# Strassen's scheme for the input products of a feed-forward layer: 18 of 22 gate and up pairs as seven quarter products

## The chip, the cores and the metric

The kernel runs on one core of a Trainium2 chip. What counts is the time of one execution on the device, in microseconds (us); the median over several runs is given. The core's engines are called by their short names: PE is TensorE (PEld its weight loads), DVE is VectorE, ACT is ScalarE, POOL is GpSimd, and SP is the queue that issues the transfers. PE writes its products into PSUM, which has eight banks; one bank holds one tile of 128 partitions by 512 float32 columns.

## The reference, cut to what matters

Two layers, each a half-step feed-forward network (FFN), a mixer (a convolution module in layer 0, a gated DeltaNet in layer 1), and a second FFN: four FFNs in all. The change touches the two of layer 1. With SEQ = 512 tokens, D_MODEL = 1024 and D_FF = 2816, each computes

```python
def swiglu_ffn(h, w_in, w_out):
    gate, up = jnp.split(h @ w_in, 2, axis=-1)
    return (jax.nn.silu(gate) * up) @ w_out

h = modulated(x, 0)
x = x + FFN_RES_WEIGHT * gate(0) * swiglu_ffn(h, w_ffn_in[i, 0], w_ffn_out[i, 0])
```

The change concerns `h @ w_in` alone: 1024 inputs by 5632 outputs (2816 gates, 2816 ups) for 512 tokens.

## The kernel before, in words

**Precision.** All operands are float32, and every product is made from halves: an operand is rounded to a type that PE takes in one pass (`whi`, `hh`), and the rest is kept beside it (`wlo`, `hl`). `mm3` (L171 to L175) then makes three matmuls for one block of 128 inputs: `whi` by `hh`, `whi` by `hl`, `wlo` by `hh`. Lines L173, L174 and L175 are those three, wherever in the program they are called from.

**Weights.** `load_raw` (L154) issues one transfer on SP for a block of 1024 inputs by 128 outputs (512 KB) into one of three `raw` buffers. `split_w` (L160) makes `whi` on ACT (L164) and `wlo` on DVE (L165), each in one of four buffers. The class `Feed` (L474) runs this as a pipeline: `load` takes the next source, `prep` splits the oldest raw block and issues the next load, `take` gives the oldest split block to PE.

**One FFN.** `ffn` (L493) works through 22 pairs of blocks, pair j being gate block j and up block j (128 gates and 128 ups), in three groups of 7, 7 and 8. `block` (L525) preps the feed, takes one split weight block, and accumulates its 8 input blocks, 24 matmuls of 512 columns, in one PSUM tile `mm`. For each pair the gate block is made, then `glu_a` (L533) takes silu on ACT; the up block is made, then `glu_b` (L537) multiplies on DVE, and `glu_c` (L541) splits the result into `ahi` (ACT) and `alo` (DVE). After a group comes its part of the output product: 8 blocks of 7 or 8 inputs, each added to `x` on DVE (L471, L464). The last two blocks of the last group lie in `tail` (L220), which already makes the next stage's first products, as 256-column halves (`head_k`). So an FFN starts with three blocks made: gate and up of pair 0 and gate of pair 1 (`begun`).

**Order.** Within `ffn` the schedule is written out by hand (`manual_schedule`): every engine, SP included, executes in the order in which the program calls it. The waits between the engines come from the framework, by the tiles that an instruction reads and writes.

**Layer 0** also pumps the modulation weights through DVE during its FFNs; in layer 1 that is over. POOL has nothing to do in the FFNs of layer 1 but one weight split in each tail (L217).

Of the kernel before, what the change touches and what calls it, by code (L numbers as in the profile page):

```python
# [15 lines left out]
P = 128  # L16
T = 512
H2 = T // 2
D = 1024
KT = D // P  # L20
NG = T // P
FF = 2816
NPAIR = FF // P
# [24 lines left out]
CT = [3,5]  # L48
ARB = 3
PAD = (40, 168)  # L50
SNW = 7
XP = ((0, 1), (1, 1), (2, 2), (4, 2), (6, 2))
WARM = (4, 7, 4)
# [54 lines left out]
def trunk_kernel(ctx: ExitStack, tc: tile.TileContext, x_in, c_in, vecs, consts, w_ada, w_st,  # L108
                 w_fi, w_fo, w_glu, w_tz, w_pw, w_dn, w_do, out):
    nc = tc.nc  # L110
    pe, act, dve, pool = nc.tensor, nc.scalar, nc.vector, nc.gpsimd

    keep = ctx.enter_context(tc.tile_pool(name="keep", bufs=1))
    wp = ctx.enter_context(tc.tile_pool(name="wp", bufs=4))
# [15 lines left out]
    def scratch(tag, shape=(P, T), dt=F32, bufs=1):  # L130
        return sc.tile(list(shape), dt, tag=tag, name=nm(tag), bufs=bufs)
# [4 lines left out]
    hh = keep.tile([P, KT, T], F32R, name="hh")  # L136
    hl = keep.tile([P, KT, T], F32R, name="hl")
# [335 lines left out]

    class Feed:  # L474
        def __init__(self, srcs, ready, go):
            self.srcs, self.ready, self.raws = list(srcs), list(ready), []
            for _ in range(3 if go else 0):
                self.load()

        def load(self):  # L480
            if self.srcs:
                src, nk = self.srcs.pop(0)
                self.raws.append((load_raw(src, nk), nk))

        def prep(self):
            if self.raws and len(self.ready) < 4:
                self.ready.append(split_w(*self.raws.pop(0)))
                self.load()

# [3 lines left out]
    def ffn(layer, which, nxt, first=None):  # L493
        sub = 2 * which
        f = layer * 2 + which
        norm = Norm()
        ng = len(GROUPS)
        with tc.tile_pool(name=nm("ffn"), bufs=1) as ap, ExitStack() as ax:
            ap.tile([P, PAD[layer]], F32, tag="pad", name=nm("pad"))
            pump = bool(ada["plan"])  # L500
            rate = APACE[which]
            if pump:
                ada["raw"] = ax.enter_context(tc.tile_pool(name=nm("adar"), bufs=2))
            done = SNW if first else len(edge["w"])
            srcs, starts = [], []
            j0 = 0
            for n in GROUPS:
                starts.append(j0)
                srcs += [(w_fi[f, i], KT) for i in range(max(2 * j0, done), 2 * (j0 + n))]
                srcs += [(w_fo[f, m, :, j0:j0 + n, :], n) for m in range(KT)]  # L510
                j0 += n
            srcs += [(s, KT) for s in (nxt[2][:2] if nxt else [])]
            feed = Feed(srcs, [] if first else edge["w"][len(edge["ps"]):], not first)
            begun = first(f, ap, feed) if first else edge["ps"]
            region = ax.enter_context(ExitStack())
            region.enter_context(tc.manual_schedule(engines=ENG))
            box = {}
            for _ in range(2):
                feed.prep()

            def step(n):
                if pump:
                    ada_step(n)

            def block(nk, mhi, mlo):  # L525
                feed.prep()
                w = feed.take()
                ps = mm_tile()
                for k in range(nk):
                    mm3(ps, w, k, mhi[:, k, :], mlo[:, k, :], k == 0, k == nk - 1)  # L530
                return ps

            def glu_a(g):  # L533
                box["s"] = s = scratch("sil", bufs=2)
                act.activation(s, g, AF.Silu)  # L535

            def glu_b(u):  # L537
                box["pr"] = pr = scratch("t", bufs=2)
                dve.tensor_tensor(pr, box["s"], u, ALU.mult)  # L539

            def glu_c(jj):  # L541
                pr = box["pr"]
                act.copy(ahi[:, jj, :], pr)  # L543
                dve.tensor_tensor(alo[:, jj, :], pr, ahi[:, jj, :].bitcast(F32), ALU.subtract)  # L544

            for gi, n in enumerate(GROUPS):
                ahi = ap.tile([P, n, T], F32R, tag="ahi", name=nm("ahi"))
                alo = ap.tile([P, n, T], F32R, tag="alo", name=nm("alo"))
                for jj in range(n):
                    if len(begun) > 1:  # L550
                        g, u = begun.pop(0), begun.pop(0)
                        glu_a(g)
                    else:
                        g = begun.pop(0) if begun else block(KT, hh, hl)
                        step(rate[0])
                        glu_a(g)
                        u = block(KT, hh, hl)
                        step(rate[1])
                    glu_b(u)
                    glu_c(jj)  # L560

                if gi == ng - 1:
                    ev = resid(norm, layer, sub)
                    for m in range(KT - 2):
                        ps = block(n, ahi, alo)
                        step(rate[2])
                        ev(ps, m, full)
                    if pump:
                        ada_drain(which == 1)
                    tail(None, n, ahi, alo, layer, sub, norm, nxt, feed)  # L570
                else:
                    ev = plain_resid(layer, sub)
                    for m in range(KT):
                        ps = block(n, ahi, alo)
                        step(rate[2])
                        ev(ps, m, full)
# [970 lines left out]
    start = ExitStack()  # L1547
# [37 lines left out]
    def begin(f, ap, feed):  # L1585
        stage = ap.tile([P, 4 * D + 2 * SNW * P], F32, tag="ahi", name="stage")
        wst = ap.tile([P, 6 * SNW * P], F32R, tag="alo", name="wst")
        NW = SNW * P
        adas, raws, ws, xn, hf = {}, {}, {}, {}, {}
# [62 lines left out]
        unit(0)  # L1652
        ps = [mm_tile() for _ in range(SNW)]
        lower(0)
        for k in range(KT):
# [132 lines left out]
```

## Time and profile before

| | us |
|---|---|
| median of 3 runs (lowest, highest) | 2051.25 (2049.03, 2054.36) |
| the profiled execution's own time | 2053.78 |
| its span in the profile | 2052.0 |
| PE busy in the span | 1999.5 (97%) |
| DVE, ACT, POOL busy | 1173.2 (57%), 788.8 (38%), 198.6 (10%) |

The profile is one execution. Times are in microseconds from the start of its span unless marked ns. A group's row has the line, the engine, the operation, the output and the inputs with their shapes, the count, then the busy time and the mean duration of one in ns, then the idle time of the engine just before such instructions and what ended it. A timeline row has the start, the duration, the engine, the line and the operation; "x8" marks eight neighbours merged into one row, from the first start to the last end. Matmuls overlap, so the duration of one is longer than the step from one start to the next; the step is what PE can do.

### The profile page before, as it was taken

To read this page: it belongs to the slowest core of one execution; us is meant where nothing else is said; L and a number is where in the kernel's file an instruction comes from. 1 tells how busy PE (TensorE), PEld (TensorE's weight loads), DVE (VectorE), ACT (ScalarE), POOL (GpSimd) and SP (SyncE) were. 2 spreads that over 40 slices of the span, in tenths; PEclk is the share of its full clock that TensorE was granted. 3 is DMA by queue.
4 is the path that set the end of the run, shared out by engine and by line. 5 is a ranking of instruction groups with operands and counts; after the bars stand their busy time and mean duration, and the time that the engine had idled before them with its cause. 6 is when DMAs were issued, how large, how long until landed. Compare 5 with 4: busy or idle time off the path is not lost.

```text
span 2052.0 us, 26228 instructions
## 1 busy us (share of the span) xinstructions
PE 1999.5 (97%) x10355; PEld 1676.0 (82%) x10355; DVE 1173.2 (57%) x1818; ACT 788.8 (38%) x1356; POOL 198.6 (10%) x140
## 2 busy tenths in 40 slices
PE   8999999998899999999999999999899999999998
PEld 6888888877898888889888888887677898888887
DVE  7767666798865656536333333676745664333334
ACT  6422222574642222324222222476656643222222
POOL 0000000299100000000000000024210100000000
PEclk9999999999899999999999999999899999999999
DMA  8767766322236656432332323322111133333331
GB/s 306 233 226 237 229 235 221 104 83 83 78 109 196 210 192 213 162 93 82 98 108 89 106 93 93 113 80 75 62 53 42 51 105 100 106 92 95 102 93 62
DMA packets 78477, 262.06 MB, mean 128 GB/s; under 512 B 8337, under 2 KB 14097, under 8 KB 78226
## 3 DMA queue, kind: packets, MB, share of 16 engines
q1 hardware_dynamic: 77810, 259.87, 39.5%
q8 instruction: 81, 1.33, 0.3%
q10 hardware_dynamic: 544, 0.52, 0.1%
q14 instruction: 42, 0.34, 0.1%
HBM read 254.59 MB, written 5.77 MB: 127 GB/s over the span
## 4 chain that ended last, share of the span: by engine, by line
PE 87%; DVE 5%; POOL 3%; ACT 3%; issue 2%; DMA 0%; SPq 0%; DVEq 0%; POOLq 0%; ACTq 0%
PE mm L173 26%; PE mm L174 26%; PE mm L175 26%; POOL pacc L674 3%; PE mm L1441 1%; PE mm L1463 1%; DVE x L1183 1%; PE aux L378 1%; PE mm L1449 1%; PE mm L1672 1%; PE mm L1673 1%; PE mm L1676 1%; PE mm L1431 1%; DVE t L1104 1%; DVE x L1188 1%
## 5 line engine op out<-in xcount | busy, mean ns | idle before, releaser
L173 PE MATMUL mm<-hh,whi 128*128 128x512 f32 (+1 forms) x1968 | 742.2, 378 | 5.3 <-ACT hh L274 3.6
L174 PE MATMUL mm<-hl,whi 128*128 128x512 f32 (+1 forms) x1968 | 736.7, 375 | 1.6 <-DVE hl L278 1.3
L175 PE MATMUL mm<-hh,wlo 128*128 128x512 f32 (+1 forms) x1968 | 735.0, 374 | 1.9 <-DVE wlo L165 1.9
L165 DVE TENSOR_TENSOR wlo<-raw,whi 128x1024 fp32r<-128x1024 f32 (+1 forms) x291 | 356.0, 1225 | 304.2 <-ACT whi L164 298.1
L173 PEld LDWEIGHTS mm<-hh,whi 128*128 128x128 f32 x1968 | 371.5, 189 | 73.8 <-ACT hh L274 4.4
L175 PEld LDWEIGHTS mm<-hh,wlo 128*128 128x128 f32 x1968 | 372.1, 189 | 68.8 <-DVE wlo L165 2.9
L174 PEld LDWEIGHTS mm<-hl,whi 128*128 128x128 f32 x1968 | 372.3, 189 | 67.3 <-DVE hl L278 3.5
L164 ACT CAST whi<-raw 128x1024 fp32r<-128x1024 f32 (+1 forms) x291 | 297.1, 1022 | 282.2 <-PE mm L174 255.5
L173 PE MATMUL mm<-ahi,whi 128*128 128x512 f32 (+1 forms) x768 | 286.4, 373 | 0.0
L174 PE MATMUL mm<-alo,whi 128*128 128x512 f32 (+1 forms) x768 | 285.7, 372 | 0.0
L175 PE MATMUL mm<-ahi,wlo 128*128 128x512 f32 (+1 forms) x768 | 285.6, 372 | 0.0
L543 ACT CAST ahi<-t 128x512 fp32r<-128x512 f32 x88 | 54.8, 623 | 371.6 <-DVE t L539 371.6
L173 PEld LDWEIGHTS mm<-ahi,whi 128*128 128x128 f32 x768 | 145.2, 189 | 25.2
L174 PEld LDWEIGHTS mm<-alo,whi 128*128 128x128 f32 x768 | 145.2, 189 | 25.0
L175 PEld LDWEIGHTS mm<-ahi,wlo 128*128 128x128 f32 x768 | 145.2, 189 | 24.9
L427 DVE CUSTOM_DVE_ANT_0 ajunk<-araw,cs 128x1024 bf16<-128x1024 f32 x128 | 156.0, 1219 | 0.6
L535 ACT ACTIVATE sil<-mm 128x512 f32<-128x512 f32 x88 | 52.6, 598 | 252.8 <-PE mm L175 252.7
L539 DVE TENSOR_TENSOR t<-sil,mm 128x512 f32<-128x512 f32 x88 | 60.4, 686 | 142.5 <-PE mm L175 140.9
L471 DVE SCALAR_TENSOR_TENSOR x<-mm,gate,x 128x512 f32<-128x512 f32 x64 | 48.1, 751 | 130.2 <-PE mm L175 130.2
L544 DVE TENSOR_TENSOR alo<-t,ahi 128x512 fp32r<-128x512 f32 x88 | 60.9, 692 | 60.6 <-ACT ahi L543 60.6
L217 POOL TENSOR_TENSOR wlo<-raw,whi 128x1024 fp32r<-128x1024 f32 x6 | 14.4, 2393 | 834.0 <-ACT whi L216 834.0
L674 POOL TENSOR_TENSOR pacc<-pacc,pr 128x492 f32<-128x492 f32 (+11 forms) x58 | 83.2, 1435 | 11.4 <-ACT pr L673 7.3
(266 smaller groups left out, 1690.6 us busy)
## 6 DMA issues: line engine op xcount, KB each, us to landing
raw<-in_w_fi_dram SPq DMA_DIRECT2D x169, 512.0 KB, 3.5
araw<-in_w_ada_dram SPq DMA_DIRECT2D x128, 512.0 KB, 4.6
raw<-in_w_fo_dram SPq DMA_DIRECT2D x64, 448.0 KB, 3.4
raw<-in_w_dn_dram SPq DMA_DIRECT2D x33, 512.0 KB, 3.7
raw<-in_w_fo_dram SPq DMA_DIRECT2D x32, 512.0 KB, 3.5
stage<-in_w_ada_dram SPq DMA_DIRECT2D x16, 512.0 KB, 6.4
raw<-in_w_glu_dram SPq DMA_DIRECT2D x16, 512.0 KB, 3.5
raw<-in_w_pw_dram SPq DMA_DIRECT2D x8, 512.0 KB, 3.7
```

What stands on the lines that cost most here:

```text
L164: act.copy(whi[:, :nk, :], raw[:, :nk, :])
L165: dve.tensor_tensor(wlo[:, :nk, :], raw[:, :nk, :], whi[:, :nk, :].bitcast(F32), ALU.subtract)
L173: pe.matmul(ps, whi[:, k, :], mhi, start=first, stop=False)
L174: pe.matmul(ps, whi[:, k, :], mlo, start=False, stop=False)
L175: pe.matmul(ps, wlo[:, k, :], mhi, start=False, stop=last)
L427: dve.tensor_tensor_reduce(junk, raw, ada["cs"], 1.0, 0.0, ALU.mult, ALU.add, accum_out=mod[:, layer, col:col + 1])
L471: dve.scalar_tensor_tensor(x[:, m, sl], ps, gate[:, j:j + 1], x[:, m, sl], ALU.mult, ALU.add)
L535: act.activation(s, g, AF.Silu)
L539: dve.tensor_tensor(pr, box["s"], u, ALU.mult)
L543: act.copy(ahi[:, jj, :], pr)
L544: dve.tensor_tensor(alo[:, jj, :], pr, ahi[:, jj, :].bitcast(F32), ALU.subtract)
L674: pool.tensor_tensor(pacc[m][:, c], pacc[m][:, c], pr[:, c], ALU.add)
```

## The change

In both FFNs of layer 1, pairs 4 to 21 go another way (`LEAD`); pairs 0 to 3 stay as they are. Take the pair's 256 outputs by 1024 inputs by 512 tokens as a product of 2 by 2 quarters: weights g1, g2 (gate, inputs 0 to 511 and 512 to 1023) and u1, u2 (up), activations by input half and by token half (l, r). Seven quarter products replace eight. Each, `prod`, has 4 input blocks by 3 matmuls of 256 columns, that is 12 matmuls. In PE's order, with three PSUM tiles Y, X, Z per pair, and under the names P0 to P6 that the prediction uses:

- P0 into Y's left half: g1 by h(lower, l). ACT copies it out (`p1`).
- P1 into X's left half: the weight sum s1 = u1 + u2 by T0. ACT copies it out (`p5`).
- P2 onto Y's left half: s2 = s1 - g1 by T1. ACT copies the sum out (`u2`).
- P3 into Z's left half: g2 by h(upper, l). DVE adds `p1` to it in place; called ZL here.
- P4 onto Y's left half: s3 = g1 - u1 by T2. ACT copies the sum out (`u3`).
- P5 onto X's left half: s4 = g2 - s2 by h(upper, r).
- DVE writes Y's right half, `u3` + `p5`; called YR here.
- P6 onto Y's left half: u2 by T3. DVE writes Z's right half, X + `u2`; called ZR here. Then silu of Z (`glu_a`), while `glu_b` and `glu_c` are put off (`late`) until after P0 of the next pair.

T0 to T3 are sums of the activations, made once per FFN by `sums_h` in four tasks (each 2 adds of 512 columns on POOL, 4 subtractions of 256 and 2 of 512 columns on DVE, 2 copies on ACT) during pairs 0 to 3. The weight sums of the next pair are made by `sums_w` in four steps, called between the products of the pair before: s1 and s3 on POOL, s2 and s4 on DVE, the splits of g, s1, s2, s3, s4 and u2 on ACT and DVE. Such a pair is called a full pair below. For the last pair of a group the steps prep weights of the output product instead (`feed.prep`); the weight sums for a group's first pair are made during the last two output blocks of the group before, and for pair 4 during pair 3. `Feed` no longer preps a block that is marked for this way (`held`); the last step issues the two next loads.

```diff
+LEAD = {(1, 0): 4, (1, 1): 4}
...
         def prep(self):
-            if self.raws and len(self.ready) < 4:
+            if self.raws and len(self.ready) < 4 and not self.held():
...
             def block(nk, mhi, mlo):
...
+                for _ in range(min(len(side), 1)):
+                    side.pop(0)()
                 return ps
...
+            def sums_h(th, tl):
...
+                    for c in (k, k + KQ):
+                        fs.append(scratch("sq", bufs=2))
+                        pool.tensor_tensor(fs[-1], hh[:, c, :].bitcast(F32), hl[:, c, :].bitcast(F32), ALU.add)
...
+                def first():
+                    st["g"], st["u"] = g, u = feed.pop(), feed.pop()
+                    st["s1"] = s1 = raw_s("pr")
+                    pool.tensor_tensor(s1, u[:, :KQ, :], u[:, KQ:, :], ALU.add)
+                def second():
...
+                    act.copy(gh, g)
+                    dve.tensor_tensor(s2, s1, g[:, :KQ, :], ALU.subtract)
+                    low(gl, g, gh)
+                    act.copy(h1[:, 0], s1)
+                    act.copy(h1[:, 1], s2)
+                def third():
...
+                    pool.tensor_tensor(s3, g[:, :KQ, :], u[:, :KQ, :], ALU.subtract)
+                    act.copy(uh[:, :KQ, :], u[:, KQ:, :])
+                    dve.tensor_tensor(s4, g[:, KQ:, :], s2, ALU.subtract)
+                    low(l1[:, 0], s1, h1[:, 0])
+                    low(l1[:, 1], s2, h1[:, 1])
+                    low(ul[:, :KQ, :], u[:, KQ:, :], uh[:, :KQ, :])
+                    act.copy(h2[:, 0], s3)
+                    act.copy(h2[:, 1], s4)
+                def fourth():
...
+                    low(l2[:, 0], s3, h2[:, 0])
+                    low(l2[:, 1], s4, h2[:, 1])
+                    feed.load()
+                    feed.load()
...
+            def seven(w, th, tl, jj, prep):
...
+                Y, X, Z = mm_tile(), mm_tile(), mm_tile()
+                y, e = Y[:, l], X[:, l]
...
+                prod(0, y, H_(lo4, l), 0)
+                settle()
+                prep[0]()
+                prod(1, e, T_(0), 0)
+                act.copy(p1, y)
+                prep[1]()
+                prod(2, y, T_(1), 1)
+                act.copy(p5, e)
+                prod(3, Z[:, l], H_(hi4, l), 2)
+                act.copy(u2, y)
+                dve.tensor_tensor(Z[:, l], Z[:, l], p1, ALU.add)
+                prep[2]()
+                prod(4, y, T_(2), 1)
+                prod(5, e, H_(hi4, r), 3)
+                act.copy(u3, y)
+                dve.tensor_tensor(Y[:, r], u3, p5, ALU.add)
+                prep[3]()
+                prod(6, y, T_(3), 3)
+                dve.tensor_tensor(Z[:, r], e, u2, ALU.add)
+                glu_a(Z)
+                def rest():
+                    glu_b(Y)
+                    glu_c(jj)
+                late.append(rest)
...
             for gi, n in enumerate(GROUPS):
...
                 for jj in range(n):
+                    if starts[gi] + jj >= lead:
+                        w, nxw = nxw["w"], {}
+                        if jj < n - 1:
+                            prep = sums_w(nxw)
+                        else:
+                            prep = (no, feed.prep, feed.prep, feed.prep)
+                        seven(w, th, tl, jj, prep)
+                        continue
```

## Rows read from the trace of the kernel before

**Rows 1.** The page: the busy time of the engines (us, share of the span, instructions), and the chain of work that ended last.

```profile
PE 1999.5 (97%) x10355; PEld 1676.0 (82%) x10355; DVE 1173.2 (57%) x1818; ACT 788.8 (38%) x1356; POOL 198.6 (10%) x140
PE 87%; DVE 5%; POOL 3%; ACT 3%; issue 2%; DMA 0%; SPq 0%; DVEq 0%; POOLq 0%; ACTq 0%
```

**Rows 2.** Busy time by stretch: the blocks of the two FFNs of layer 1, from the first whole block to the tail. Columns: length, busy time of each engine with the count of its instructions, PE's granted clock (1.00 is full speed, 2.4 GHz), share of the DMA engines, GB/s.

```profile
967.40:1303.00 335.60, 335.60 (x1498) 278.51 (x1497) 128.14 (x137) 94.75 (x118) 0.00 (x0) 1.00 0.33 99
1690.40:2037.00 346.60, 346.60 (x1590) 289.51 (x1588) 131.37 (x146) 96.32 (x123) 0.00 (x0) 1.00 0.30 90
```

**Rows 3.** Timeline of PE: two matmuls of 512 columns that lie 48 matmuls apart, one pair.

```profile
1099.99 0.39 PE L173 MATMUL mm<-hh,whi 128*128 128x512 f32 x1
...
1110.87 0.39 PE L173 MATMUL mm<-hh,whi 128*128 128x512 f32 x1
```

**Rows 4.** Timeline of PE at the start of the first of these FFNs: two matmuls of 256 columns that lie 42 matmuls apart, and the first of the block behind them.

```profile
961.96 0.28 PE L173 MATMUL mm<-hh,whi 128*128 128x256 f32 x1
...
967.00 0.28 PE L173 MATMUL mm<-hh,whi 128*128 128x256 f32 x1
...
967.36 0.40 PE L173 MATMUL mm<-hh,whi 128*128 128x512 f32 x1
```

**Rows 5.** Timeline of DVE at the start of the first of these FFNs: two independent subtractions with nothing between them.

```profile
967.80 2.36 DVE L165 TENSOR_TENSOR wlo<-raw,whi 128x1024 fp32r<-128x1024 f32 x2 [3.41 <-ACT whi L164]
```

**Rows 6.** Groups of instructions of DVE, ACT and POOL over the whole span, each shape apart.

```profile
L165 DVE TENSOR_TENSOR wlo<-raw,whi 128x1024 fp32r<-128x1024 f32 x227 | 286.1, 1262 | 254.0 <-ACT whi L164 250.0
L165 DVE TENSOR_TENSOR wlo<-raw,whi 128x896 fp32r<-128x896 f32 x64 | 69.9, 1092 | 50.2 <-ACT whi L164 48.0
L544 DVE TENSOR_TENSOR alo<-t,ahi 128x512 fp32r<-128x512 f32 x88 | 60.9, 692 | 60.6 <-ACT ahi L543 60.6
L539 DVE TENSOR_TENSOR t<-sil,mm 128x512 f32<-128x512 f32 x88 | 60.4, 686 | 142.5 <-PE mm L175 140.9 <-ACT sil L535 1.5
L273 DVE SCALAR_TENSOR_TENSOR mm<-x,gain,aux 128x256 f32<-128x256 f32 x80 | 38.5, 487 | 3.1 <-PE aux L378 1.5
L407 DVE TENSOR_TENSOR ssum<-ssum,sq 128x256 f32<-128x256 f32 x36 | 15.1, 420 | 8.4 <-ACT sq L402 8.2
...
L164 ACT CAST whi<-raw 128x1024 fp32r<-128x1024 f32 x227 | 236.8, 1045 | 171.9 <-PE mm L174 168.4 <-DMA raw<-in_w_pw_dram 2.1 <-DMA raw<-in_w_fi_dram 1.4
L543 ACT CAST ahi<-t 128x512 fp32r<-128x512 f32 x88 | 54.8, 623 | 371.6 <-DVE t L539 371.6
L535 ACT ACTIVATE sil<-mm 128x512 f32<-128x512 f32 x88 | 52.6, 598 | 252.8 <-PE mm L175 252.7
L897 ACT CAST hh<-sil 128x256 fp32r<-128x256 f32 x16 | 6.5, 408 | 0.5
```

**Rows 7.** Timelines of POOL and DVE in the convolution module, where POOL adds (two operands from SBUF) while DVE subtracts (two operands from SBUF).

```profile
409.58 1.25 POOL L674 TENSOR_TENSOR pacc<-pacc,pr 128x490 f32<-128x490 f32 x1
...
410.91 2.10 POOL L674 TENSOR_TENSOR pacc<-pacc,pr 128x489 f32<-128x489 f32 x1
...
409.88 2.03 DVE L165 TENSOR_TENSOR wlo<-raw,whi 128x1024 fp32r<-128x1024 f32 x1 [0.43 <-ACT whi L164]
```

**Rows 8.** Timelines of PE, ACT and DVE in the DeltaNet, at two PSUM tiles that PE fills in column slices and another engine reads slice by slice: four transposes into `aux` and the first read of its first slice; eight matmuls into `mm` (two for each of four slices) and the first read of its first slice.

```profile
1377.58 0.60 PE L1125 MATMUL aux<-cst,sil 128*128 128x128 f32 x4
...
1378.28 0.28 ACT L1048 ACTIVATE sqj<-aux 128x128 bf16<-128x128 f32 x1
...
1515.95 1.16 PE L1449 MATMUL mm<-sil,kt 64*128 64x128 f32 x8
...
1517.14 0.29 DVE L1452 COPY so<-mm 128x128 f32<-128x128 f32 x1 [4.24 <-PE mm L1449]
```

**Rows 9.** Timelines around three hand-overs: the last matmul of a 256-column block and the DVE instruction that waits for it; a DVE result and the weight load that waits for it; the first two 256-column matmuls after a break.

```profile
937.62 0.28 PE L175 MATMUL mm<-ahi,wlo 128*128 128x256 f32 x1
...
937.95 0.48 DVE L249 SCALAR_TENSOR_TENSOR x<-mm,gate,x 128x256 f32<-128x256 f32 x1 [0.67 <-PE mm L175]
...
1525.13 0.36 DVE L1434 SCALAR_TENSOR_TENSOR sq<-mm,nbe,vb 64x128 f32<-64x128 f32 x1
...
1525.54 0.13 PEld L1441 LDWEIGHTS mm<-sq,rm 64*64 64x64 f32 x1 [0.45 <-DVE sq L1434]
...
943.50 0.36 PE L173 MATMUL mm<-ahi,whi 128*128 128x256 f32 x1
943.71 0.28 PE L174 MATMUL mm<-alo,whi 128*128 128x256 f32 x1
```

**Rows 10.** The page's DMA issues: the weight loads of the input product (count, size of one, median us from issue to landing).

```profile
raw<-in_w_fi_dram SPq DMA_DIRECT2D x169, 512.0 KB, 3.5
```

More of the change, by code (lines that the diff above doesn't have):

```diff
@@ L50 @@
 PAD = (40, 168)
+KQ = KT // 2
+LEAD = {(1, 0): 4, (1, 1): 4}
 SNW = 7
@@ L478, in __init__, with held @@
                 self.load()
+        def held(self):
+            return self.raws[0][1] < 0
         def load(self):
@@ L504, in ffn @@
             done = SNW if first else len(edge["w"])
+            lead = LEAD.get((layer, which), NPAIR)
             srcs, starts = [], []
@@ L508, in ffn @@
                 starts.append(j0)
-                srcs += [(w_fi[f, i], KT) for i in range(max(2 * j0, done), 2 * (j0 + n))]
+                srcs += [(w_fi[f, i], -KT if i >= 2 * lead else KT) for i in range(max(2 * j0, done), 2 * (j0 + n))]
                 srcs += [(w_fo[f, m, :, j0:j0 + n, :], n) for m in range(KT)]
@@ L523, in step @@
                     ada_step(n)
+            side = []
             def block(nk, mhi, mlo):
@@ L544, in glu_c, with task @@
                 dve.tensor_tensor(alo[:, jj, :], pr, ahi[:, jj, :].bitcast(F32), ALU.subtract)
+            def sums_h(th, tl):
+                def task(k):
+                    tf = [scratch("pr", (P, 2, H2), bufs=2) for _ in range(2)]
+                    fs = []
+                    for c in (k, k + KQ):
+                        fs.append(scratch("sq", bufs=2))
+                        pool.tensor_tensor(fs[-1], hh[:, c, :].bitcast(F32), hl[:, c, :].bitcast(F32), ALU.add)
+                    t1, t2, t3, t4 = (tf[i // 2][:, i % 2, :] for i in range(4))
+                    l, r = halves
+                    dve.tensor_tensor(t1, fs[0][:, r], fs[0][:, l], ALU.subtract)
+                    dve.tensor_tensor(t3, fs[1][:, r], fs[0][:, r], ALU.subtract)
+                    dve.tensor_tensor(t2, fs[1][:, r], t1, ALU.subtract)
+                    dve.tensor_tensor(t4, fs[1][:, l], t2, ALU.subtract)
+                    for i in range(2):
+                        c = slice(2 * i, 2 * i + 2)
+                        act.copy(th[:, c, k, :], tf[i])
+                        dve.tensor_tensor(tl[:, c, k, :], tf[i], th[:, c, k, :].bitcast(F32), ALU.subtract)
+                return [lambda k=k: task(k) for k in range(KQ)]
@@ new lines, in ffn, with settle, T_, H_ @@
+            late = []
+            def settle():
+                while late:
+                    late.pop(0)()
+            def seven(w, th, tl, jj, prep):
+                l, r = halves
+                lo4, hi4 = slice(0, KQ), slice(KQ, KT)
+                def T_(i):
+                    return th[:, i], tl[:, i]
+                def H_(ks, sl):
+                    return hh[:, ks, sl], hl[:, ks, sl]
+                def prod(i, ps, m, ends):
+                    (whi, wlo), (mhi, mlo) = w[i], m
+                    for k in range(KQ):
+                        pe.matmul(ps, whi[:, k, :], mhi[:, k, :], start=ends in (0, 2) and k == 0, stop=False, skip_group_check=True)
+                        pe.matmul(ps, whi[:, k, :], mlo[:, k, :], start=False, stop=False, skip_group_check=True)
+                        pe.matmul(ps, wlo[:, k, :], mhi[:, k, :], start=False, stop=ends in (2, 3) and k == KQ - 1, skip_group_check=True)
+                Y, X, Z = mm_tile(), mm_tile(), mm_tile()
+                y, e = Y[:, l], X[:, l]
+                pp = scratch("ssum").rearrange("p (a n) -> p a n", a=2)
+                uu = scratch("t", bufs=2).rearrange("p (a n) -> p a n", a=2)
+                p1, p5, u2, u3 = pp[:, 0], pp[:, 1], uu[:, 0], uu[:, 1]
+                prod(0, y, H_(lo4, l), 0)
[22 more added lines that the diff above has]
+                late.append(rest)
@@ L546, in ffn, with no @@
+            def no():
+                pass
             for gi, n in enumerate(GROUPS):
@@ L548, in ffn @@
                 alo = ap.tile([P, n, T], F32R, tag="alo", name=nm("alo"))
-                for jj in range(n):
+                if gi == 0 and lead < NPAIR:
+                    th = ap.tile([P, 4, KQ, H2], F32R, tag="th", name=nm("th"))
+                    tl = ap.tile([P, 4, KQ, H2], F32R, tag="tl", name=nm("tl"))
+                    side += sums_h(th, tl)
+                    side.pop(0)()
+                    nxw = {}
+                    s4 = sums_w(nxw)
+                    side += [lambda: (s4[0](), s4[1]()), lambda: (s4[2](), s4[3]())]
+                for jj in range(n):
+                    if starts[gi] + jj >= lead:
[6 more added lines that the diff above has]
+                        continue
                     if len(begun) > 1:
@@ L560, in ffn @@
                     glu_c(jj)
+                settle()
                 if gi == ng - 1:
@@ L573, in ffn @@
                     for m in range(KT):
+                        if m == KT - 2 and lead < NPAIR:
+                            nxw = {}
+                            s4 = sums_w(nxw)
+                            side += [lambda: (s4[0](), s4[1]()), lambda: (s4[2](), s4[3]())]
                         ps = block(n, ahi, alo)
```

34 lines of the change are left out of this document (33 added, 1 removed).

## The prediction, made before the changed kernel was run

> **What bounds the kernel now.** I read the page first: PE is busy for 97% of the span and carries 87% of the chain that ended last [rows 1]. Then the stretches that the change touches: in the blocks of both layer-1 FFNs PE is busy for all of 335.6 and 346.6 us, at a granted clock of 1.00, while DVE works 128 and 131 us, ACT 95 and 96, and POOL nothing [rows 2]. So there the time is the number of PE's matmuls times their step, and nothing else waits long enough to matter. The steps come from the timeline. With 512 columns, 48 matmuls, one pair, take 1110.87 - 1099.99 = 10.88 us, 0.2267 each [rows 3]. With 256 columns, 42 matmuls take 967.00 - 961.96 = 5.04 us, 0.120 each [rows 4]: more than half of 0.2267, so part of the scheme's eighth is lost in the halving. Both levels are full clock, and the pauses below are far under a microsecond, so I charge nothing for the clock.
>
> **The change, part by part.**
>
> *PE's own work.* A changed pair is 7 x 12 = 84 matmuls of 256 columns: 84 x 0.120 = 10.08 us against 10.88, a gain of 0.80. Over 18 pairs and two FFNs that would be 36 x 0.80 = 28.8 us. This is the ceiling.
>
> The Trainium skill (TensorE: Matmul & The Clock Gate, Back-to-back issue gap) gives a matmul N / 2.4 + 2.5 ns: 109 ns for 256 columns and 216 ns for 512, and by it I would estimate 10.36 - 9.17 = 1.19 us a pair. The trace shows 120 and 227 ns, some 11 ns more on each, and the rows decide.
>
> *Loads of the other engines in a full pair.* One DVE instruction starts 0.09 before the one before it has ended: two of 1.225 take 2.36 [rows 5, 6]. A full pair gives DVE one subtraction of 1024 columns (1.23), eight of 512 (0.69), one product (0.69) and three adds of 256 (0.42) [rows 6]: 8.7 us, less 13 x 0.09, is 7.5. ACT has 1.05 + 6 x 0.62 + 4 x 0.41 + 0.60 = 7.0, less 12 x 0.09, about 5.9; POOL two adds of 1.25 [rows 7]. All are below 10.08, so no engine is full. What counts is the order in DVE's queue.
>
> *The wait that the change adds.* P6 adds to the left half of tile Y; YR, on DVE, writes its right half and comes before P6 in the program. If waits go by whole PSUM tiles, P6 must wait for YR. The trace of before has no write beside a write, but it shows reads: ACT reads the first of four transposed slices at 1378.28, 0.10 after the fourth was written (1377.58 + 0.60), not after the first; DVE reads the first of four slices at 1517.14, just after the last of eight matmuls (1515.95 + 1.16) [rows 8]. Both go by the whole tile, so I take the same for a write. The bounds are no wait at all and the wait that I now work out.
>
> Count from P0's start. P3's last matmul starts at 48 x 0.12 - 0.12 = 5.64, and a waiting DVE instruction starts 0.33 after such a start (937.62 to 937.95) [rows 9]: ZL at 5.97. DVE is free by then (its instruction before, the split of g, ends near 4.8). In the queue behind ZL (0.42 - 0.09 = 0.33) stand s4, two splits of s1 and s2, and the split of u2, 4 x 0.60 = 2.40, and only then YR: it starts at 8.70 and ends at 9.12. Its operand `u3` is no later: s4 ends at 6.99, ACT copies it until 7.65, and `u3` is done near 8.0. P6 is due at 6 x 1.44 = 8.64. A weight load starts 0.05 after the DVE result that it waited for (1525.13 + 0.36 to 1525.54), and after a break the first matmul's step is 0.20 in place of 0.12 [rows 9]. So P6 is late by 9.12 + 0.05 + 0.08 - 8.64 = 0.61, and a full pair takes 10.69: a gain of 0.19, not 0.80. With ZL and YR at the 0.49 of the nearest row that writes PSUM (L273, [rows 6]) it would be 0.05.
>
> The Trainium skill (PSUM — Partial Sum Buffer, PSUM bank collisions raise a hardware error) says that PE's write and DVE's write in one bank must not meet, whatever their columns, and that waits are to go by bank and not by address. By that P6 waits and the pair is 10.69; by columns it would not wait and the pair is near 10.25 (below). The rows on reads lean the same way; no row shows two writers.
>
> *Is a second wait behind it?* After YR come two splits, so ZR runs 10.23 to 10.65, silu on ACT 10.69 to 11.29, the product on DVE 11.32 to 12.01, then the copy of `ahi` from 12.04, and behind it in ACT's queue `p1`, 12.57 to 12.98. The next P2 needs `p1` at 10.69 + 2.88 = 13.57. No second wait, 0.6 to spare.
>
> *Transfers and POOL.* As many loads as before, each later: u of the pair after next may land only after s4 has freed its buffer, at 6.99. At 3.5 us a load [rows 10] it lands at 10.5, about when the next pair starts; POOL's s1 and s3 then run until 2.4 and are far from the stretch 5.97 to 9.12.
>
> *Last pairs of a group* (6 in all). DVE has one split of 896 columns (1.09) between ZL and YR: free at 7.30. ACT's `u3` follows P4 (last start 7.08 + 0.33) and is done at 7.82; YR ends at 8.27, before 8.64. The whole 0.80 is gained. The late silu, product and split end some 2.5 us after P6; the last input block of the next output product is needed 18 x 0.227 = 4.1 us after it, so they are hidden.
>
> *Pairs 0 to 3.* PE runs five whole blocks there, 5 x 5.44 = 27.2 us from 967.36 [rows 4]. DVE gets four tasks of `sums_h` (4 x 0.33 + 2 x 0.60 = 2.5 each), one `sums_w` (7 x 0.60 + 1.14 = 5.3), four weight splits (4.6) and four products with splits (4.8): 24.8 us, plus waits for ACT's copies. That ends near 995, at the start of pair 4, whose first late part is needed 1.4 us later. POOL's adds can push it: free or up to 2 us per FFN; I take 0.5 each. The weight sums made in the last two output blocks of a group (5.3 us on DVE beside 9.5 of PE) cost nothing.
>
> *Sum.* 30 full pairs (15 per FFN) x 0.19 = 5.7, 6 last pairs x 0.80 = 4.8, less 1.0: 9.5 us. The profiled execution's own time is 2053.78 (its span 2052.0 and 1.8 around it), which lies 2.5 over the median of 2051.25; from it 2044.3 follows, and for the median 2041.7, say 2042.
>
> **Rivals.**
> - *No wait at P6* (waits by columns, or YR earlier than I think). Then the chain through ZR, silu, product, `ahi` and `p1` decides: it reaches P2 0.15 late and shifts the whole pair, 10.25. 30 x 0.63 + 4.8 - 1.0 = 22.7: 2028.5. For it speaks only that the halves are disjoint; rows 8 speak against it.
> - *The full pairs gain nothing.* The window from ZL to YR holds six DVE instructions; 0.03 more on each (a longer add into PSUM, a wait that is handled apart) takes the 0.19 away: 4.8 - 1.0 gained, 2047.5, up to 2052 with twice that.
> - *Slower: POOL in the window.* A POOL add and a DVE instruction with two SBUF operands do not run together: DVE's 1.23 became 2.03 and ended 1.08 after POOL's add did, and POOL's next add took 2.10 in place of 1.25 [rows 7]. If s3 falls between 5.97 and 9.12, DVE stands for 0.85 to 1.25 and P6 with it: the pair takes 11.5 to 11.9, 30 x (0.66 to 1.06) - 3.8 = 16 to 28 us more, 2067 to 2079. It decides from a landing time of about 7 us, twice the median; against it speak 3.5 us and a DMA share of 0.30 [rows 2, 10].
>
> **How the numbers follow.** The forecast, a wait of about 0.6 at P6, has a chance of 0.55, with a range of its own of 2036 to 2050. No wait 0.15, nothing gained in the full pairs 0.17, POOL in the window 0.13. About 0.3% (6 us) is what a measurement can tell here: faster means under 2045.1. Seven tenths of the forecast (0.39) and the first rival give 0.54; the rest of the forecast and the second give 0.33; the third 0.13. The range reaches down to the first rival and up past the second, 2027 to 2055, and leaves out the third.
>
> **What would show it.** Steps of 0.120 within a product; P6's first weight load released by DVE's YR, some 0.6 late, in the pairs that are not last in a group, and no such break in the last; a pair of 10.7 and 10.1 us; POOL's adds in the first 3 us of a pair. Wrong would be: a step above 0.1295 (the break-even, 10.88 / 84), breaks at P2 or P4, DVE's subtractions stretched to 1.5 us, or PE's clock below 1.00.

## The result, and the profile after

The changed kernel takes 2060.64 us (median of 6 runs, 2058.75 to 2062.15) against 2051.55 for the kernel before in 6 runs beside it. The ratio is 1.0042 with a 95% interval of 1.0029 to 1.0055: some 9 us slower. I had forecast 2042 and a range that ended at 2055.

The line numbers of the changed kernel: a product is L661 to L663, ZL is L680, YR L685, ZR L688; `sums_h` adds on POOL in L565 and works on DVE in L568 to L571 and L575; the splits of `sums_w` on DVE are L583, and ACT's split of g is L600; `glu_b` is L552, the copy of `ahi` L556, `alo` L557, `p1` L674. The page, for [rows 1]:

```profile
PE 1982.2 (96%) x11651; PEld 1718.2 (83%) x11651; DVE 1373.2 (67%) x2190; ACT 904.7 (44%) x1660; POOL 317.5 (15%) x228
PE 77%; DVE 11%; ACT 4%; issue 4%; POOL 3%; DMA 1%; SPq 0%; DVEq 0%; POOLq 0%; ACTq 0%
```

PE is busy for 17 us less, but the chain that ended last runs 11% through DVE where it had 5%. The windows of [rows 2], and the few microseconds behind the start of pair 4:

```profile
967.40:1303.00 335.60, 324.67 (x2121) 297.54 (x2120) 225.67 (x321) 149.34 (x267) 56.34 (x42) 0.99 0.33 99
1690.40:2037.00 346.60, 335.93 (x2207) 308.53 (x2207) 231.60 (x334) 154.04 (x274) 59.53 (x44) 0.99 0.30 90
...
997.00:1003.80 6.80, 5.34 (x23) 5.04 (x24) 6.12 (x10) 3.88 (x8) 0.99 (x1) 0.50 0.47 133
```

PE was busy in all of the first two stretches and is now idle for 11 us in each; in the third line the granted clock is 0.50, the lower of its two levels (1.2 GHz).

**A full pair goes as forecast.** Timelines of PE, DVE and PE's weight loads in pair 8, from P0's first matmul to that of the next pair:

```profile
1081.77 0.28 PE L661 MATMUL mm<-hh,whi 128*128 128x256 f32 x1
...
1087.73 0.43 DVE L680 TENSOR_TENSOR mm<-mm,ssum 128x256 f32<-128x256 f32 x1 [1.04 <-PE mm L663]
...
1090.47 0.43 DVE L685 TENSOR_TENSOR mm<-t,ssum 128x256 f32<-128x256 f32 x1
...
1090.95 0.19 PEld L661 LDWEIGHTS mm<-th,whi 128*128 128x128 f32 x1 [0.59 <-DVE mm L685]
...
1092.49 0.28 PE L661 MATMUL mm<-hh,whi 128*128 128x256 f32 x1
```

ZL starts 5.96 after the pair's start and YR 8.70; P6's first weight load waits for YR; the pair takes 10.72 (forecast: 5.97, 8.70, 10.69). The last pairs of a group take 10.08, as forecast. Of the 15 full pairs of an FFN 14 gain 0.155 each, 2.2 us, and the three last ones 2.4.

**Pair 4 does not.** Timelines of PE, ACT and DVE where pairs 0 to 3 end:

```profile
992.88 0.39 PE L177 MATMUL mm<-hh,wlo 128*128 128x512 f32 x1
995.95 0.39 PE L661 MATMUL mm<-hh,whi 128*128 128x256 f32 x1 [2.68 <-ACT whi L600]
996.18 0.28 PE L662 MATMUL mm<-hl,whi 128*128 128x256 f32 x1
998.40 0.58 PE L663 MATMUL mm<-hh,wlo 128*128 128x256 f32 x1 [1.94 <-DVE wlo L583]
998.77 0.42 PE L661 MATMUL mm<-hh,whi 128*128 128x256 f32 x1
998.99 0.42 PE L662 MATMUL mm<-hl,whi 128*128 128x256 f32 x1
...
1007.59 0.39 PE L661 MATMUL mm<-th,shi 128*128 128x256 f32 x1 [0.79 <-ACT t L679]
...
994.33 0.62 ACT L556 CAST ahi<-t 128x512 fp32r<-128x512 f32 x1 [1.44 <-DVE t L552]
994.86 1.04 ACT L600 CAST whi<-raw 128x1024 fp32r<-128x1024 f32 x1
...
992.41 1.29 DVE L575 TENSOR_TENSOR tl<-pr,th 128x512 fp32r<-128x512 f32 x2 [0.23 <-ACT th L574]
993.62 0.68 DVE L552 TENSOR_TENSOR t<-sil,mm 128x512 f32<-128x512 f32 x1
994.99 1.62 DVE L557 TENSOR_TENSOR alo<-t,ahi 128x512 fp32r<-128x512 f32 x1 [0.69 <-ACT ahi L556]
...
997.13 1.21 DVE L583 TENSOR_TENSOR wlo<-raw,whi 128x1024 fp32r<-128x1024 f32 x1
```

Read it backwards. PE's first weight load of pair 4 waits for ACT's split of g; ahead of that in ACT's queue stands the copy of `ahi`, which waits for DVE's product; ahead of the product on DVE stands the last task of `sums_h`. Then P0's third matmul waits for DVE's split of g. From one start to the next 3.07 and 2.22 us pass, where a step alone is 0.23 and 0.12. After these PE's clock falls, and the step is 0.21 to 0.22 in place of 0.120. A third pause, 1.07 from start to start, comes at P4, which waits for ACT's copy `u2` (L679). In ACT's queue that stands behind the split of s2, and s2 is late on DVE. Pair 4 takes 16.20 us, in the second FFN 16.17. With the pause ahead of it, 3.07 - 0.23 = 2.84, that is 2.84 + 16.2 - 10.72 = 8.3 us more per FFN than a full pair, 8.2 more than a pair of before (the expectations below say 8.5, which counts the whole 3.07). The other pairs gain 4.6, so 3.6 are lost per FFN and 7.2 in both, of the 9.1 measured. The timelines agree: from the first whole block of an FFN to the last product of its tail it takes 344.1 us before and 347.7 after, in both.

**Why DVE is late.** Timelines of DVE and POOL in the third task of `sums_h`:

```profile
985.89 0.42 DVE L568 TENSOR_TENSOR pr<-sq 128x256 f32<-128x256 f32 x1
...
987.01 1.40 DVE L571 TENSOR_TENSOR pr<-sq,pr 128x256 f32<-128x256 f32 x1
988.34 2.38 DVE L575 TENSOR_TENSOR tl<-pr,th 128x512 fp32r<-128x512 f32 x2
...
986.72 1.41 POOL L565 TENSOR_TENSOR sq<-hh,hl 128x512 f32<-128x512 f32 x1 [4.76 <-DVE pr L569]
988.58 1.58 POOL L565 TENSOR_TENSOR sq<-hh,hl 128x512 f32<-128x512 f32 x1 [0.46 <-DVE pr L571]
```

The two POOL adds of the next task start as soon as DVE has freed their buffers, that is in the middle of this task. The DVE instructions beside them take 1.40 for 0.42 and 2.38 for 1.29. This is what [rows 7] show, called the lock from here on: an add on POOL and a DVE instruction with two SBUF operands do not run together. It strikes three tasks in each FFN; the last task, with no add behind it, took 0.43 and 1.29. POOL's weight sums s1 and s3 bring it too. Ahead of pair 4 `alo`, at 994.99 above, takes 1.62 in place of 0.69, and in pair 4 s2 takes 1.78 in place of 0.68, just ahead of the pause at P4. The Trainium skill (SBUF — State Buffer, Who interferes with whom) says that a DVE instruction with two SBUF inputs and a GpSimd instruction that reads SBUF exclude each other, and that the order of issue decides which stands. These rows agree: 0.42 grows by 0.98 beside an add of 1.41 that had begun first.

### The profile page after: what moved, and what is told of

The parts are those of the page before. It is cut to its first block, busy times and chain, and to the rows that moved or that the text cites. A ratio compares the mean times of both kernels' runs of the same rounds, so it can differ in the third digit from the quotient of the medians.

```text
span 2057.8 us, 29707 instructions
## 1 busy us (share of the span) xinstructions
PE 1982.2 (96%) x11651; PEld 1718.2 (83%) x11651; DVE 1373.2 (67%) x2190; ACT 904.7 (44%) x1660; POOL 317.5 (15%) x228
## 4 chain that ended last, share of the span: by engine, by line
PE 77%; DVE 11%; ACT 4%; issue 4%; POOL 3%; DMA 1%; SPq 0%; DVEq 0%; POOLq 0%; ACTq 0%
PE mm L175 19%; PE mm L176 19%; PE mm L177 19%; PE mm L661 5%; PE mm L663 4%; PE mm L662 4%; POOL pacc L849 3%; DVE slo L583 2%; DVE sq L617 1%; DVE wlo L583 1%; PE mm L1616 1%; DVE x L1358 1%; PE mm L1638 1%; PE mm L1624 1%; PE aux L380 1%
## 5 line engine op out<-in xcount | busy, mean ns | idle before, releaser
L175 PE MATMUL mm<-hh,whi 128*128 128x512 f32 (+1 forms) x1392 | 518.9, 374 | 6.2 <-ACT hh L276 4.4
L176 PE MATMUL mm<-hl,whi 128*128 128x512 f32 (+1 forms) x1392 | 513.1, 369 | 1.6 <-DVE hl L280 1.3
L177 PE MATMUL mm<-hh,wlo 128*128 128x512 f32 (+1 forms) x1392 | 511.2, 368 | 1.8 <-DVE wlo L167 1.8
L167 DVE TENSOR_TENSOR wlo<-raw,whi 128x1024 fp32r<-128x1024 f32 (+1 forms) x219 | 267.8, 1224 | 156.3 <-ACT whi L166 152.1
L175 PEld LDWEIGHTS mm<-hh,whi 128*128 128x128 f32 x1392 | 263.4, 190 | 51.9 <-ACT hh L276 5.5
L177 PEld LDWEIGHTS mm<-hh,wlo 128*128 128x128 f32 x1392 | 264.2, 190 | 46.3 <-DVE wlo L167 2.9
L176 PEld LDWEIGHTS mm<-hl,whi 128*128 128x128 f32 x1392 | 264.4, 190 | 45.1 <-DVE hl L280 3.7
L176 PEld LDWEIGHTS mm<-alo,whi 128*128 128x128 f32 x768 | 144.8, 189 | 24.9
L177 PEld LDWEIGHTS mm<-ahi,wlo 128*128 128x128 f32 x768 | 144.7, 188 | 24.9
L556 ACT CAST ahi<-t 128x512 fp32r<-128x512 f32 x88 | 54.7, 622 | 223.7 <-DVE t L552 223.7
L661 PE MATMUL mm<-th,shi 128*128 128x256 f32 x432 | 124.3, 288 | 1.5 <-ACT t L679 1.3
L662 PE MATMUL mm<-tl,shi 128*128 128x256 f32 x432 | 123.7, 286 | 0.0
L663 PE MATMUL mm<-th,slo 128*128 128x256 f32 x432 | 123.6, 286 | 0.0
L557 DVE TENSOR_TENSOR alo<-t,ahi 128x512 fp32r<-128x512 f32 x88 | 76.9, 873 | 60.5 <-ACT ahi L556 60.5
```

The source lines that it names most:

```text
L661: pe.matmul(ps, whi[:, k, :], mhi[:, k, :], start=ends in (0, 2) and k == 0, stop=False, skip_group_check=True)
L662: pe.matmul(ps, whi[:, k, :], mlo[:, k, :], start=False, stop=False, skip_group_check=True)
L663: pe.matmul(ps, wlo[:, k, :], mhi[:, k, :], start=False, stop=ends in (2, 3) and k == KQ - 1, skip_group_check=True)
```

## The experiments

The theory after the result: the entry to pair 4 costs 8.3 us per FFN because DVE is late there, and DVE is late by POOL's lock. Rivals: its load alone, or the switch to 256 columns itself. Beside it, P6's wait: is it the shared PSUM tile and YR's place in the queue?

**One more plain pair** (`lead5`).

```diff
-LEAD = {(1, 0): 4, (1, 1): 4}
+LEAD = {(1, 0): 5, (1, 1): 5}
...
                     s4 = sums_w(nxw)
+                    side += [no] * (2 * (lead - 4))
                     side += [lambda: (s4[0](), s4[1]()), lambda: (s4[2](), s4[3]())]
```

> Five plain pairs in place of four; the sums of the weights stay in the last two plain blocks, so DVE has 10.9 us more of PE's time for the same sums and only one product with its splits more. Theory (DVE comes to the first changed pair late, behind the sums of the activations): the two idle stretches of PE at the entry (3.07 and 2.22 us) and the 6.8 us at half clock behind them go, 8.5 us per FFN, so 2 x 8.5 less 2 x 0.16 for a pair that is not changed: about 17 us below the changed kernel, 2044. Rival (the break comes with the first changed pair wherever it stands, from the switch to products of 256 columns): idle and half clock move along with the entry, 2061.

Measured 2049.56 (10 runs, 2047.25 to 2051.17), ratio to before 0.9988 (0.9979 to 0.9998). The idle ahead of the first changed pair is gone, and the clock stays at full speed. From PE's timeline, the windows and ACT's timeline:

```profile
1003.87 0.39 PE L177 MATMUL mm<-hh,wlo 128*128 128x512 f32 x1
1004.10 0.28 PE L661 MATMUL mm<-hh,whi 128*128 128x256 f32 x1
...
1007.81 0.39 PE L661 MATMUL mm<-th,shi 128*128 128x256 f32 x1 [0.68 <-ACT ssum L674]
...
1004.00:1018.00 14.00, 12.64 (x102) 12.10 (x101) 12.14 (x18) 6.74 (x14) 2.98 (x2) 1.00 0.48 137
...
1006.86 0.62 ACT L556 CAST ahi<-t 128x512 fp32r<-128x512 f32 x1 [2.67 <-DVE t L552]
1007.39 0.37 ACT L674 COPY ssum<-mm 128x256 f32<-128x256 f32 x1
```

The rival of the switch falls. But 11 us came back and not 17: the first changed pair still takes 12.1 to 12.3, because P2 waits for `p1`, behind the copy of `ahi`, behind a product that DVE makes late, and P4 is 0.8 to 1.1 late for `u2`, with s2 again at 1.78 beside s3. DVE is still behind, only less.

**The split of u2 behind YR** (`ul_late`).

```diff
                     low(l1[:, 1], s2, h1[:, 1])
-                    low(ul[:, :KQ, :], u[:, KQ:, :], uh[:, :KQ, :])
...
+                    st["u2"] = u[:, KQ:, :]
                 def fourth():
...
+                    uh, ul = st["uw"]
+                    low(ul[:, :KQ, :], st["u2"], uh[:, :KQ, :])
                     l2 = fresh("slo")
```

> Four plain pairs as in the changed kernel; the split of the right half of u moves from ahead of YR to behind it in DVE's queue, so YR starts 0.6 us earlier. Theory (P6 waits for YR, and YR for the queue): the break ahead of P6 goes, a full pair takes 10.1 to 10.25 in place of 10.72, 30 pairs gain 14 to 18 us; the entry stays as it is: 2043 to 2047. Rival (P6 waits for the operand u3 or for something else than its place in the queue): P6 stays 0.6 late, 2061.

Measured 2046.26 (7 runs), ratio to before 0.9973 (0.9962 to 0.9984): 14.4 us below the changed kernel. In pair 8, which starts at 1082.16 (timelines of DVE and PE; a product is L663 to L665 and YR L687 here):

```profile
1090.36 0.43 DVE L687 TENSOR_TENSOR mm<-t,ssum 128x256 f32<-128x256 f32 x1
...
1090.80 0.28 PE L665 MATMUL mm<-hh,slo 128*128 128x256 f32 x1
1090.92 0.30 PE L663 MATMUL mm<-th,whi 128*128 128x256 f32 x1
...
1092.37 0.28 PE L663 MATMUL mm<-hh,whi 128*128 128x256 f32 x1
```

YR starts 8.20 after the pair's start, no break stands ahead of P6, and the pair takes 10.21; others go up to 10.24. The prediction's first rival had worked out 10.25 for a pair without this wait. The entry is as before: 3.06 and 2.22 us of idle. One DVE instruction of 0.6 us, moved by one place, is worth 14 us here, since 28 pairs hang on it.

**No adds on POOL** (`no_pool`).

```diff
-                        fs.append(scratch("sq", bufs=2))
-                        pool.tensor_tensor(fs[-1], hh[:, c, :].bitcast(F32), hl[:, c, :].bitcast(F32), ALU.add)
+                        fs.append(hh[:, c, :].bitcast(F32))
```

> The sums of the activations take the high halves alone, so POOL's eight adds per FFN fall away and with them the low halves of the sums (that part of the computation is left out). DVE keeps every instruction that it had. Theory (POOL's adds lock DVE's instructions with two SBUF operands): the stretched ones (1.40 and 2.38 us) fall back to 0.42 and 1.29, DVE gains 2.1 us in each of three tasks, the first split of pair 4 is there 6 us earlier, the idle at the entry and the half clock go, 2044. Rival (DVE is late by its load alone, 25 us of instructions in 27 us): the same durations, the same 3 us of idle, 2061.

Measured 2050.01, one run. DVE's timeline in the third task and at g's split, then PE's at P2 of pair 4 (lines one lower than in the changed kernel):

```profile
981.16 0.42 DVE L567 TENSOR_TENSOR pr<-hh 128x256 f32<-128x256 f32 x1
...
982.28 0.42 DVE L570 TENSOR_TENSOR pr<-hh,pr 128x256 f32<-128x256 f32 x1
982.94 1.29 DVE L574 TENSOR_TENSOR tl<-pr,th 128x512 fp32r<-128x512 f32 x2 [0.23 <-ACT th L573]
...
990.71 1.21 DVE L582 TENSOR_TENSOR wlo<-raw,whi 128x1024 fp32r<-128x1024 f32 x1
...
997.11 0.38 PE L660 MATMUL mm<-th,shi 128*128 128x256 f32 x1 [2.23 <-ACT ssum L673]
```

The stretched instructions are back to 0.42 and 1.29. In the changed kernel DVE waits for none of POOL's results in these tasks, so what goes with the adds is not such a wait. A task takes 3.06 from its first subtraction to its last in place of 4.83. From DVE's first weight split of the stage (964.26 here, 966.32 in the changed kernel) to the end of g's split it is 27.7 us in place of 32.0, and the idle ahead of P0 is gone. But pair 4 still takes 15.40 and 14.73: P2 starts 2.5 us after the matmul before it, since it waits for `p1`. So neither theory holds alone. The lock of these adds is 4.0 of the 8.3 us per FFN (16.2 less 15.1, the mean of the two, and the 2.84), and DVE's load, with the waits for ACT's copies between, is the rest. In that rest is still the lock beside s1 and s3 (`alo` 1.67, s2 1.76 here), which no run took away; 4.0 is the share of the eight adds and not of the lock as a whole. The time is 10.6 below the changed kernel, of which these rows show some 7.9.

**The adds on DVE** (`dve_adds`).

```diff
-                        pool.tensor_tensor(fs[-1], hh[:, c, :].bitcast(F32), hl[:, c, :].bitcast(F32), ALU.add)
+                        dve.tensor_tensor(fs[-1], hh[:, c, :].bitcast(F32), hl[:, c, :].bitcast(F32), ALU.add)
```

> The eight adds of 512 columns that POOL makes for the sums of the activations stand on DVE. DVE gets 0.6 to 0.7 us more for each, 3.6 to 4.2 in the three tasks after the first, and loses the lock. By the lock theory it saves 2.1 in each of the three, 6.3, so the first split of pair 4 comes 2 to 2.7 us earlier, the first idle at the entry shrinks from 3.1 to about 1 us: 4 to 12 us below the changed kernel, 2049 to 2057. By the load theory it comes 3.6 to 4.2 us later and PE's idle grows by as much in each FFN: 2067 or more.

Measured 2061.61 (4 runs), ratio to before 1.0047 (1.0032 to 1.0062): the changed kernel's time. Both forecasts missed. The rows, PE's timeline and DVE's:

```profile
994.75 0.39 PE L177 MATMUL mm<-hh,wlo 128*128 128x512 f32 x1
998.21 0.38 PE L661 MATMUL mm<-hh,whi 128*128 128x256 f32 x1 [3.08 <-ACT whi L600]
...
991.69 1.29 DVE L565 TENSOR_TENSOR sq<-hh,hl 128x512 f32<-128x512 f32 x2
...
999.39 1.21 DVE L583 TENSOR_TENSOR wlo<-raw,whi 128x1024 fp32r<-128x1024 f32 x1
```

The subtractions of the sums take 0.42 and 1.29 here too, though every sum is made: the stretch comes with the adds on POOL. From the first split (968.19) to the end of g's split it takes 32.4 us, against 32.0: two adds cost DVE 1.2 us a task, and the lock had cost 1.77 in each of three tasks, in part hidden in the first, where DVE waits for silu anyway. By the lock DVE paid for POOL's adds about what it pays for making them itself.

**YR away from the PSUM tile** (`yr_sbuf`).

```diff
-                dve.tensor_tensor(Y[:, r], u3, p5, ALU.add)
+                dve.tensor_tensor(p1, u3, p5, ALU.add)
...
-                    glu_b(Y)
+                    box["pr"] = pr = scratch("t", bufs=2)
+                    dve.tensor_tensor(pr[:, l], box["s"][:, l], y, ALU.mult)
+                    dve.tensor_tensor(pr[:, r], box["s"][:, r], p1, ALU.mult)
```

> YR stands at the same place of DVE's queue, behind the same four subtractions, but writes an SBUF buffer (that of p1, which is dead by then) in place of the right half of the PSUM tile into whose left half P6 adds; the product with silu is made in two halves. Theory (P6 waits for YR because both write one PSUM tile): the break ahead of P6 goes although YR is as late as before; what is left is the chain ZR, silu, product, copy, p1, which reaches P2 0.1 to 0.2 late: a full pair of 10.2 to 10.3 in place of 10.72, some 13 to 15 us below the changed kernel, 2046 to 2048. Rival (P6 waits for ACT's copy u3 of the tile that it adds to, or for an operand): P6 stays 0.6 late, 2060 or more. The entry stays as it is.

Measured 2052.37 (10 runs), ratio to before 1.0004 (0.9995 to 1.0013). In pair 8, which starts at 1081.42, timelines of DVE, PE and ACT (YR is L686, the two halves of the product L694 and L695):

```profile
1090.67 0.42 DVE L686 TENSOR_TENSOR ssum<-t,ssum 128x256 f32<-128x256 f32 x1
...
1090.49 0.28 PE L663 MATMUL mm<-hh,slo 128*128 128x256 f32 x1
1090.61 0.28 PE L661 MATMUL mm<-th,whi 128*128 128x256 f32 x1
...
1095.39 0.39 PE L661 MATMUL mm<-th,shi 128*128 128x256 f32 x1 [0.31 <-ACT ssum L675]
...
1093.30 0.42 DVE L694 TENSOR_TENSOR t<-sil,mm 128x256 f32<-128x256 f32 x1 [0.66 <-ACT sil L548]
1093.64 0.77 DVE L695 TENSOR_TENSOR t<-sil,ssum 128x256 f32<-128x256 f32 x1
...
1094.97 0.37 ACT L675 COPY ssum<-mm 128x256 f32<-128x256 f32 x1
```

P6 starts 0.12 behind the matmul before it, and before YR has even begun. So it was the shared tile that made P6 wait. (The edit also takes the buffer of `p1` and `p5` later, behind P0.) The size was missed: the product in two halves takes 1.11 us in place of 0.69 (its second half has two SBUF operands and stretches to 0.77 beside POOL), `p1` is late by as much, and P2 waits 0.3 to 0.6 in most pairs. One wait had only been traded for another.

**The weight sums one block earlier** (`lead5_early`).

```diff
-LEAD = {(1, 0): 4, (1, 1): 4}
+LEAD = {(1, 0): 5, (1, 1): 5}
...
+                    side += [no] * 1
```

> Five plain pairs, and the sums of the weights one block earlier than with five plain pairs before, so that the last plain pair's product stands ahead of no weight sums in DVE's queue. Theory (what was left at the entry, P2 0.84 late in both FFNs and P4 0.84 to 1.08, is p1: ACT's copy p1 stands behind the copy of the last plain pair's product, and that product on DVE behind seven splits of the weights): both go, the first changed pair takes 10.7 like the others, 2 x 1.4 to 1.6 us less than 2049.6: 2046 to 2047. Rival (it is the first changed pair's own load, its sums beside those of the next pair): stays at 12.1 to 12.3, 2049.6.

Measured 2049.09 (10 runs), ratio 0.9987 (0.9978 to 0.9996): no change from `lead5`, and the first changed pair takes 12.24 and 12.55. The theory falls: from 989 to 1009 DVE waits for nothing but ACT's copies, so another order only changes which work is late. That DVE carries a backlog there, whatever its order, is the theory of the last run below.

**Edits together** (`early_ul`: `lead5_early` and `ul_late`).

> The three edits together that have been looked at one by one: five plain pairs, the sums one block earlier, and the split of the right half of u behind YR. If entry and P6 are separate causes they add: no idle at the entry, 34 changed pairs of 10.1 to 10.23 in place of 10.88: 34 x 0.67 = 23 below the kernel before, 2029; if P6's break only covers another, 2040 or more.

Measured 2035.77 (4 runs), ratio 0.9921 (0.9908 to 0.9935). The two causes add: 11.6 and 14.4 below the changed kernel alone, 24.9 together. The full pairs take 10.11 to 10.24. About half of what is missing to 2029 is the first changed pair, still 12.0 in both FFNs; the rest was not followed.

**Two more splits behind ZR** (`early_both`).

```diff
-                prep[3]()
                 prod(6, y, T_(3), 3)
                 dve.tensor_tensor(Z[:, r], e, u2, ALU.add)
                 glu_a(Z)
+                prep[3]()
```

> As the run before, and the two splits of s3 and s4 also move, behind ZR, so that silu, product, the copy of it and p1 come 1.2 us earlier. Theory (the 0.1 that is left at P2 is the chain through ZR, silu, product, copy and p1): a changed pair takes 10.08, only its matmuls; 34 x 0.80 = 27 below the kernel before: 2024 to 2026. Rival (the splits are then late for P4 of the next pair, or the product stands behind them): a pair stays at 10.2 or longer, 2029 or more.

Measured 2035.34 (5 runs), ratio 0.9922 (0.9908 to 0.9935): the same. The wait at P2 is gone, but one of 0.15 has come at P4, for `u2`: ACT's copies `p5` and `u2` stand behind its split of s2.

**That split behind u2** (`h1_later`: `early_both` and this).

```diff
                     act.copy(h1[:, 0], s1)
-                    act.copy(h1[:, 1], s2)
...
+                    act.copy(h1[:, 1], s2)
                     act.copy(uh[:, :KQ, :], u[:, KQ:, :])
```

> The last kernel with one more edit: ACT's split of s2 stands behind the copies p5 and u2 in ACT's queue and no longer ahead of them. What is left of a wait in a full pair of the last kernel is 0.15 ahead of P4 (its first weight load waits for u2, u2 stands behind the split of s2, and that waits 0.6 for s2 on DVE). Theory: it goes, a full pair takes 10.08, 26 pairs gain 0.1 to 0.15: 2 to 4 us less, 2031 to 2033. Rival (ACT's work, not its order, makes u2 late, or the later split holds up P2's or P4's weights): 10.2 as before, 2035.3.

Measured 2032.92 (4 runs), ratio 0.9908 (0.9893 to 0.9922). A full pair takes 10.13. The rest, 0.05 at P6, was not followed.

**Six plain pairs** (`lead6`: `h1_later` with `LEAD` 6 and `[no] * 4`).

> As h1_later with six plain pairs in place of five. With five, DVE runs without a break from the sums of the activations into the first changed pair and is 1.8 us behind there, which makes the first changed pair 12.0 to 12.5. Theory (it is DVE's backlog, whatever the order within it): another plain pair gives DVE 10.9 us for 3.8 us of work, the backlog goes, the first changed pair takes 10.1 to 10.2; gained 2 x 2, lost 2 x 0.8 for a pair that is not changed: 2 us less than h1_later, about 2030. Rival (the first changed pair's own sums): it stays at 12, 1.6 us more than h1_later.

Measured 2029.37 (4 runs, 2028.93 to 2029.68), ratio 0.9890 (0.9873 to 0.9906). From PE's timeline and DVE's ahead of the first changed pair:

```profile
1015.12 0.28 PE L663 MATMUL mm<-hh,whi 128*128 128x256 f32 x1
...
1025.19 0.40 PE L175 MATMUL mm<-ahi,whi 128*128 128x512 f32 x1
...
1004.51 0.69 DVE L552 TENSOR_TENSOR t<-sil,mm 128x512 f32<-128x512 f32 x1 [1.06 <-PE mm L177]
```

DVE waits for PE again (1.06), so it has caught up, and the first changed pair takes 10.07. That P2 waits no more is the backlog's doing: `p1`, which P2 needs, stands ahead of a pair's own sums in the queues of ACT and DVE. For P4 and P6 the run does not decide: pair 6 is also the last of its group and carries no sums of a next pair. This version beats both kernels, with 32 changed pairs in place of 36: some 23 us below the kernel before, 31 below the changed one.

## Why the prediction was wrong

**The step that failed is "Pairs 0 to 3"**: "free or up to 2 us per FFN; I take 0.5 each". It was 8.3 each. With the terms as measured the sum is 4.4 for 28 full pairs and 4.8 for the last ones, less 16.3 (pair 4 and the pause ahead of it, against a pair of before, in both FFNs): 7 us lost in place of 9.5 gained. Three things stood behind it.
- The lock was in my own rows [rows 7], and I looked for it at one place only, between ZL and YR. There it never came: in the full pair shown POOL's two adds run from 1081.85 to 1084.40, in the pair's first 3 us, as I had said. (What they stretch in the full pairs is `alo`, here 1.18 for 0.69, or s2. DVE still waits 1.04 for PE ahead of ZL in the pair shown. I had not counted this stretch, so that it costs nothing there is luck.) In pairs 0 to 3, where six of the eight adds stand beside DVE's subtractions by construction, I dismissed it in half a sentence. The third rival's mechanism was right, and its place wrong.
- The waits in DVE's own list were too short as well. My 24.8 us end with pair 3's product and its split, and I left about 3 us for waits. That product ended 36.2 us after DVE's first split of the stage, and in `no_pool` 31.9, with 5.1 of waits for ACT. I asked when the first late part is needed on DVE ("1.4 us later"). What came late first was ACT's half of the split of g, needed at once: in ACT's queue it stands behind a copy that waits for DVE. DVE's half of it is needed at P0's third matmul, 0.24 after the start.
- "I charge nothing for the clock" rested on pauses far under a microsecond. The two pauses of 3.07 and 2.22 us were followed by 6.8 us at half clock. Of the 5.5 us by which pair 4 exceeds the other full pairs, 2.1 are the pause at P0's third matmul; the stretch at half clock holds 23 matmuls at some 0.09 more each, 2.1; the pause at P4 is 1.0. Of the signs named for "wrong", the breaks at P2 and P4 and the lower clock showed in these pairs, and subtractions of 1.5 us and more.

**What was right.** The steps of 0.120; the wait of P6 (0.64 for 0.61, released by YR, which starts at 8.70); the pair of 10.72 (10.69; a step of 0.21 in [rows 9] I had read as 0.20) and the last pairs of 10.08; `p1` 12.58 after the start of the pair (12.57), so no second wait; weight sums during the output blocks at no cost. `yr_sbuf` and `ul_late` show that the cause of P6's wait was the one named, and `ul_late`'s 10.21 comes close to the first rival's 10.25. The ceiling of 0.80 a pair was real too: `lead6` takes 0.75 from each full pair.

**What stays open.** What the entry would cost at full clock, or with s1 and s3 off POOL, was not shown by a run of its own; so the first changed pair's remaining 1.5 to 2 us in the runs with five plain pairs are not divided between DVE's load and that lock. The rows account for 7.2 of the 9.1 us between the medians. The two profiled executions lie 5.8 apart, so outside these FFNs the changed kernel's was 1.4 shorter; why is open, and single executions of either kernel differ by 3 to 5. The pairs of `lead6` give 24.3 us by their rows, where 22.8 were measured.

## What to carry to other kernels

Before a steady state is priced pair by pair, price its entry in the same way: list each queue in the stage that prepares it, with the waits between them, and ask which operand the first product needs at once. An engine that is idle on the page is not free: POOL's adds took from DVE about what they took off it. And when a wait is found, look for what stands ahead of the awaited instruction in its queue; here the order of a few instructions of 0.6 us and a later entry turned 9 us lost into 23 won.

## What the runs showed of the hardware that was not expected

The clock does not follow from the length of a break alone. In `no_pool` PE broke off for 2.5 us in both FFNs, between the same two products. In the first, half clock followed (998.3 to 1001.7); in the second, none. The windows of that run:

```profile
998.30:1001.70 3.40, 3.40 (x19) 3.40 (x18) 2.80 (x3) 1.94 (x6) 1.10 (x1) 0.50 0.01 5
1727.50:1734.00 6.50, 5.60 (x46) 5.32 (x45) 6.50 (x10) 3.55 (x8) 1.26 (x1) 1.00 0.23 70
```

And the lock costs both sides: POOL's add of 512 columns, 1.29 before the first task of `sums_h`, took 1.41 and 1.58 beside DVE's subtractions.
